# Attention powers turned by VectorE's 32x32 blocks and a scratch in device memory instead of TensorE transposes

## Chip, cores and metric

One core of a Trainium2 chip. The metric is the device time of one execution in microseconds; the time before is the median of three runs.

## The reference, cut to what matters

One decoder layer on x of 512 positions and 1024 channels, in float32. The normed input is projected at once into nine parts: queries, keys and values of 8 heads of 64 (with a gate), a pooling branch and a spatial gating branch (each with a gate). Of attention this matters:

```
logits = (q . k) * scale + bias(distance)      # own block of 256 causal, earlier block where selected
probs  = softmax(logits)                        # exp(logits - max) / sum
out    = probs . v                              # per head, 512 x 64
y      = concat(out_a * silu(g_a), pooled * silu(g_b), gated * silu(g_c)) @ w_out
```

Then the residual, a per-layer input embedding times a sigmoid gate, and a final norm.

## The kernel before, in words

Every float32 product is made of three matmuls of rounded parts ("hi" and "lo"). Weights come as chunks of 128x1024, fetched by `fetch` (L102) into three buffers `raw`; ScalarE makes the `hi` part (L128) and VectorE the `lo` part (L116), and 24 matmuls use one chunk. `ORDER` (L30) lists the projections; `through` runs them one by one and calls `tick` after each five matmuls. A tick advances every side chain by one step, and the attention loop by 1.4 steps on average (`RATE`).

Attention works on 32 tiles: 8 heads `h` times 4 blocks `i` of 128 queries, with n = 128 (i + 1) keys. In turn s of the loop in `attention` (L481), three steps long, tile s gets its scores (two matmuls into a PSUM bank, L408), the lowest logit (`lowest`, VectorE) and the powers (`powers`: exponentials on ScalarE, their sums by the same instruction). Tile s - 1 is divided by its sum (`normalise`: addition, reciprocal, multiplication on VectorE, L444 to L446). Tile s - 4 (`LAG`) is turned: i + 1 transposes of 128x128 by TensorE against `flip` (L457; `flip` also reverses the queries, which were projected in reverse order), a copy from PSUM into `ph` by ScalarE (L460), and the rest `pl` by VectorE (L116). When a head's four tiles are turned, `weigh` (L463) multiplies them with the values in eight matmuls into `ps_o`, and a copy and an addition put the head's output into `y`.

```
for j in range(n):
    nc.tensor.transpose(ps[:, j * P:(j + 1) * P], probs[h, i][:, j * P:(j + 1) * P], flip)
...
nc.scalar.activation(ph[:, :n, iq], src, AF.Copy)
```

The eight gate projections come last in the order. Their Silu, and the product of gate and branch, wait in side chains (`gate`, L613); `part` (L695) multiplies all gates but the last with two chunks of `w_out`, and only then the last one, so that the last gate has time. The order on each engine is set by the framework from the order of the code and from what it takes to be ready; engines work through their own order without skipping. All transfers but one half of the last output go through SP's queue. Tiles with the tag `t` (`temp`) share 15 buffers, the powers two buffers for each i.

Of the kernel before, what the change touches and what calls it, by code (L numbers as in the profile page):

```python
# [23 lines left out]
HD = 64  # L24
# [6 lines left out]
UNIT = 5  # L31
WARM = 14
PM = 4
LAG = 4
HELD = 5
RATE = 1.4
SS_AT = 2
# [15 lines left out]
def trunk(ctx: ExitStack, tc: tile.TileContext, t: dict, out: bass.AP):  # L53
    nc = tc.nc
    pool = lambda name, **k: ctx.enter_context(tc.tile_pool(name=name, **k))
    const = pool("const", bufs=1)
    wp = pool("wp", bufs=3)
    big = pool("big", bufs=1)
    gen = pool("gen", bufs=15)
    small = pool("small", bufs=4)  # L60
    dram = pool("dram", bufs=1, space=bass.MemoryType.DRAM)
    pm = pool("pm", bufs=PM, space=bass.MemoryType.PSUM)
    pa = pool("pa", bufs=8 - PM, space=bass.MemoryType.PSUM)
# [25 lines left out]
    def run(mms):  # L89
        for m in mms:  # L90
# [7 lines left out]
    stream = ([t["wv"][c] for c in range(4)] + [w for z, m in order for w in chunks[z](m)]  # L98
              + [t["wo"][m] for m in range(KD)] + [t["wpg"][e, c] for e in range(2) for c in range(4)])
    raws, parts, used = [], [], [0]  # L100

    def fetch(upto):  # L102
        while len(raws) < min(upto, len(stream)):
            raw = wp.tile([P, 1024], F32, tag="raw", name=f"raw_{len(raws)}")
            nc.sync.dma_start(raw, stream[len(raws)])
            raws.append(raw)

    last_parts, lows = [], []
# [48 lines left out]
        nc.sync.dma_start(xk[k], t["xT"][k])  # L157
    ident = const.tile([P, P], F32, name="ident")
    make_identity(nc, ident)
    flip = const.tile([P, P], F32, name="flip")  # L160
    nc.gpsimd.memset(flip, 0.0)
    nc.gpsimd.affine_select(flip, flip, pattern=[[1, P]], compare_op=ALU.not_equal, fill=1.0, base=-(P - 1), channel_multiplier=1)
    half = const.tile([P, 4], F32, name="half")
    nc.vector.memset(half, -0.5)
    ones = const.tile([P, 1], F32, name="ones")
# [67 lines left out]
    bias = []  # L233
# [85 lines left out]
    for g in range(4):  # L319
        r = slice((g % 2) * HD, (g % 2 + 1) * HD)  # L320
# [19 lines left out]
        nc.vector.reciprocal(icnt, icnt)  # L340


    qk, probs, sums, score, heads, yat = {}, {}, {}, {}, {}, {}

    def project(name):
        wh, wl = take()
# [52 lines left out]

    lim = 0.5 * BIG * 256.0 / math.sqrt(HD)  # L400

    def scores(h, i):
        qs, kh, kl = qk[h // 2][h % 2]
        n = P * (i + 1)
        nn = max(n, 256)
        ps = bank(pa, f"ps_s{h}{i}")
        iq = slice(i * P, (i + 1) * P)
        nc.tensor.matmul(ps[:, :nn], qs[:, iq], kh[:, :nn], start=True, stop=False)  # L408
        nc.tensor.matmul(ps[:, :nn], qs[:, iq], kl[:, :nn], start=False, stop=True)  # L409
        sc = gen.tile([P, n], F32, tag=f"p{i}", name=f"s_{h}{i}", bufs=2)  # L410
        st = small.tile([P, 8], F32, tag="st", name=f"st_{h}{i}", bufs=8)
        probs[h, i], sums[h, i] = sc, st
        score[h, i] = ps
        if i >= 2:
            gs = gen.tile([P, 256], BF16, tag="junk", name=f"gs_{h}{i}", bufs=2)
            nc.scalar.activation(gs, ps[:, :256], AF.Copy, accum_out=st[:, 2:3])
# [13 lines left out]

    def powers(h, i):
        n = P * (i + 1)
        sc, st = probs[h, i], sums[h, i]
        if i < 2:
            nc.scalar.activation(sc[:, :n], sc[:, :n], AF.Exp, bias=st[:, 0:1], scale=-1.0, accum_out=st[:, 1:2])  # L435
        else:
            nc.scalar.activation(sc[:, :256], sc[:, :256], AF.Exp, bias=st[:, 6:7], scale=-1.0, accum_out=st[:, 1:2])
            nc.scalar.activation(sc[:, 256:n], sc[:, 256:n], AF.Exp, bias=st[:, 0:1], scale=-1.0, accum_out=st[:, 7:8])  # L438

    def normalise(h, i):  # L440
        n = P * (i + 1)
        sc, st = probs[h, i], sums[h, i]
        if i >= 2:
            nc.vector.tensor_tensor(st[:, 1:2], st[:, 1:2], st[:, 7:8], op=ALU.add)  # L444
        nc.vector.reciprocal(st[:, 2:3], st[:, 1:2])
        nc.vector.tensor_scalar(sc[:, :n], sc[:, :n], st[:, 2:3], None, op0=ALU.mult)  # L446

    def turn(h, i):
        if i == 0:
            heads[h] = [big.tile([P, NT, 512], F32R, tag=n, name=f"{n}_{h}") for n in ("ph", "pl")]  # L450
            for z in heads[h]:
                nc.gpsimd.memset(f(z[:, 3, 256:384]), 0.0)  # L452
        ph, pl = heads[h]
        n = i + 1
        ps = bank(pa, f"ps_t{h}{i}")
        for j in range(n):
            nc.tensor.transpose(ps[:, j * P:(j + 1) * P], probs[h, i][:, j * P:(j + 1) * P], flip)  # L457
        src = ps[:, :n * P].rearrange("p (j q) -> p j q", q=P)
        iq = slice(i * P, (i + 1) * P)
        nc.scalar.activation(ph[:, :n, iq], src, AF.Copy)  # L460
        return low(ph[:, :n, iq], pl[:, :n, iq], src)

    def weigh(h):  # L463
        ph, pl = heads[h]
# [12 lines left out]

        nc.scalar.activation(y[r], ps[o], AF.Copy)
        return lambda: nc.vector.tensor_tensor(y[r], ps[r], y[r], op=ALU.add)

    def attention():  # L481
        tiles = [(h, i) for h in range(HEADS) for i in range(NT)]
        at = lambda d: tiles[d] if 0 <= d < len(tiles) else None
        add = None
        for s in range(len(tiles) + LAG + 2):
            while at(s) and len(qk.get(at(s)[0] // 2, [()])[0]) < 3:
                yield
            part = turn(*at(s - LAG)) if at(s - LAG) else None
            if add:
                add()  # L490
                add = None
            yield
            if at(s - LAG - 1) and (s - LAG) % NT == 0:
                add = weigh(at(s - LAG - 1)[0])
            if at(s):
                scores(*at(s))
            if at(s - 1):
                normalise(*at(s - 1))
            if part:
                part()  # L500
            if at(s):
                lowest(*at(s))
            yield
            if at(s):
                powers(*at(s))
            progress[0] = s + 1
            yield
# [100 lines left out]


    yh, yl = {}, {}  # L610
    y4, held, busy, credit = [], [], [], [0]

    def gate(c):  # L613
        ps, mms = project(f"g{c}")
# [90 lines left out]
    ps = [bank(pm, f"ps_h{m}") for m in range(2)]  # L705
# [94 lines left out]
    i = NT - 1  # L800
# [95 lines left out]
```

## Time and profile before

| what | value |
|---|---|
| median of 3 runs | 297.73 us (297.4 to 298.9) |
| profiled execution | 298.0 us |
| its span, first to last instruction | 296.0 us |
| mean granted TensorE clock | 0.995 |
| TensorE / VectorE / ScalarE / GpSimd busy | 286.5 / 204.3 / 178.0 / 34.0 us |
| moved by DMA | 33.26 MB, mean 112 GB/s |

PE is TensorE's matmuls, PEld its weight loads, DVE VectorE, ACT ScalarE, POOL GpSimd, SPq SyncE's queue of DMA issues. L457 is line 457 of the kernel. A tile's buffer numbers are left out, so `ps_t` is all of `ps_t00` to `ps_t73`. Matmuls overlap, so their durations sum to more than the time that they take.

### The profile page before, as it was taken

How to read it: one execution, taken by the hardware profiler on the slowest of the kernel's cores; microseconds unless marked ns; L12 is line 12 of the kernel's file. 1: busy time of each engine (PE TensorE's matmuls, PEld its weight loads, DVE VectorE, ACT ScalarE, POOL GpSimd, SP SyncE). 2: the span in 40 equal slices, each digit the busy share in tenths (PEclk: the TensorE clock that was granted, in tenths of full speed). 3: DMA queues.
4: the chain of work that ended last, by engine and by line, in shares of the span. 5: the costliest groups of instructions: out<-in, count | busy, mean ns of one | idle time of the engine just before them, and what ended most of it. 6: DMA issues, size and time to landing. Idle time of an engine off the chain costs nothing.

```text
span 296.0 us, 4201 instructions
## 1 busy us (share of the span) xinstructions
PE 286.5 (97%) x1436; PEld 240.1 (81%) x1436; DVE 204.3 (69%) x498; ACT 178.0 (60%) x364; POOL 34.0 (11%) x81
## 2 busy tenths in 40 slices
PE   8998999999999999999999999999999999999990
PEld 6876788788889988888888888888888888888890
DVE  2799798667987799978968858562654452355464
ACT  4895584567775756656699999651432332475221
POOL 2591132000001210000000000000000000051021
PEclk9999999999999999999999999999999999999998
DMA  6969734422222042222222222265233323400033
GB/s 177 331 235 267 290 116 144 142 71 71 74 72 73 0 144 71 74 71 73 71 71 71 74 72 71 73 207 218 83 132 95 117 71 117 132 36 3 1 141 142
DMA packets 12933, 33.26 MB, mean 112 GB/s; under 512 B 1896, under 2 KB 2664, under 8 KB 12912
## 3 DMA queue, kind: packets, MB, share of 16 engines
q1 hardware_dynamic: 12768, 32.74, 33.0%
q8 instruction: 11, 0.18, 0.3%
q10 hardware_dynamic: 144, 0.26, 0.2%
q14 instruction: 10, 0.08, 0.1%
HBM read 30.87 MB, written 2.12 MB: 111 GB/s over the span
## 4 chain that ended last, share of the span: by engine, by line
PE 69%; DVE 11%; ACT 9%; issue 4%; POOL 2%; DMA 2%; SPq 1%; POOLq 0%; DVEq 0%; ACTq 0%
PE ps_g L81 9%; PE ps_g L80 9%; PE ps_g L79 9%; PE ps_h L81 5%; PE ps_h L80 5%; PE ps_h L79 5%; ACT kh L388 2%; PE ps_t L457 2%; DMA x<-in_xT 2%; DVE lo L116 2%; ACT hi L128 1%; PE ps_o L474 1%; PE ps_o L473 1%; PE ps_s L409 1%; PE ps_u L81 1%
## 5 line engine op out<-in xcount | busy, mean ns | idle before, releaser
L128 ACT ACTIVATE hi<-raw 128x1024 fp32r<-128x1024 f32 x40 | 42.1, 1054 | 40.8 <-issue 29.8
L116 DVE TENSOR_TENSOR lo<-raw,hi 128x1024 fp32r<-128x1024 f32 x40 | 48.9, 1222 | 10.0 <-ACT hi L128 9.6
L81 PE MATMUL ps_g<-hn_hi,lo 128*128 128x512 f32 x64 | 25.6, 400 | 0.0
L80 PE MATMUL ps_g<-hn_lo,hi 128*128 128x512 f32 x64 | 25.4, 396 | 0.0
L79 PE MATMUL ps_g<-hn_hi,hi 128*128 128x512 f32 x64 | 25.3, 396 | 0.0
L79 PE MATMUL ps_g<-hi,h_hi 128*128 128x512 f32 (+1 forms) x52 | 19.9, 382 | 0.0
L701 DVE TENSOR_TENSOR h<-ps_h,h 128x512 f32<-128x512 f32 x8 | 5.5, 691 | 20.5 <-PE ps_h L81 20.5
L81 PE MATMUL ps_g<-hi,h_lo 128*128 128x512 f32 (+1 forms) x52 | 19.5, 374 | 0.0
L80 PE MATMUL ps_g<-lo,h_hi 128*128 128x512 f32 (+1 forms) x52 | 19.4, 373 | 0.0
L116 DVE TENSOR_TENSOR pl<-ps_t,ph 128x128 fp32r<-128x128 f32 (+3 forms) x32 | 15.5, 483 | 0.4
L460 ACT ACTIVATE ph<-ps_t 128x128 fp32r<-128x128 f32 (+3 forms) x32 | 13.7, 427 | 2.9 <-PE ps_t L457 2.6
L452 POOL MEMSET ph<- 128x128 f32 x8 | 1.9, 233 | 112.1 <-PE ps_o L473 73.9
L80 PEld LDWEIGHTS ps_g<-hn_lo,hi 128*128 128x128 f32 x64 | 12.0, 188 | 2.3
L457 PE MATMUL ps_t<-flip,s 128*128 128x128 f32 x80 | 13.9, 272 | 0.0
L81 PEld LDWEIGHTS ps_g<-hn_hi,lo 128*128 128x128 f32 x64 | 12.0, 188 | 2.2
L79 PEld LDWEIGHTS ps_g<-hn_hi,hi 128*128 128x128 f32 x64 | 12.1, 188 | 2.1
L80 PE MATMUL ps_v<-lo,hn_hi 128*128 128x512 f32 x32 | 12.7, 398 | 0.6 <-DVE lo L116 0.5
L438 ACT ACTIVATE s<-s,st 128x128 f32<-128x128 f32 (+1 forms) x16 | 7.2, 451 | 10.0 <-DVE st L428 9.8
L435 ACT ACTIVATE s<-s,st 128x128 f32<-128x128 f32 (+1 forms) x16 | 7.2, 453 | 9.9 <-DVE st L423 9.9
L457 PEld LDWEIGHTS ps_t<-flip,s 128*128 128x128 f32 x80 | 10.4, 140 | 3.0
L763 POOL TENSOR_SCALAR fg<-fg 128x1024 f32<-128x1024 f32 x1 | 3.8, 3810 | 77.7 <-ACT hi L128 77.7
L446 DVE TENSOR_SCALAR s<-s,st 128x128 f32<-128x128 f32 (+3 forms) x32 | 12.2, 384 | 0.7
(227 smaller groups left out, 860.6 us busy)
## 6 DMA issues: line engine op xcount, KB each, us to landing
raw<-in_wg SPq DMA_DIRECT2D x8, 512.0 KB, 3.3
raw<-in_wo SPq DMA_DIRECT2D x8, 512.0 KB, 3.3
raw<-in_wpg SPq DMA_DIRECT2D x8, 512.0 KB, 3.3
x<-in_xT SPq DMA_DIRECT2D x8, 256.0 KB, 5.3
raw<-in_wv SPq DMA_DIRECT2D x4, 512.0 KB, 5.8
bias<-tab_d SPq DMA_DIRECT2D x8, 256.0 KB, 6.1
raw<-in_wq SPq DMA_DIRECT2D x4, 512.0 KB, 6.8
raw<-in_wk SPq DMA_DIRECT2D x4, 512.0 KB, 3.3
```

Of the source, the lines that this page charges most:

```text
L79: return [lambda: nc.tensor.matmul(ps, lh, rh, start=first, stop=False), lambda: nc.tensor.matmul(ps, lh, rl, start=False, stop=False), la ...
L80: lambda: nc.tensor.matmul(ps, lh, rl, start=False, stop=False),
L81: lambda: nc.tensor.matmul(ps, ll, rh, start=False, stop=last)]
L116: return lambda: nc.vector.tensor_tensor(lo, raw, f(hi), op=ALU.subtract)
L128: nc.scalar.activation(hi, raws[j], AF.Copy)
L388: nc.scalar.activation(kh[e][r[z]], ps[r[e]], AF.Copy)
L435: nc.scalar.activation(sc[:, :n], sc[:, :n], AF.Exp, bias=st[:, 0:1], scale=-1.0, accum_out=st[:, 1:2])
L438: nc.scalar.activation(sc[:, 256:n], sc[:, 256:n], AF.Exp, bias=st[:, 0:1], scale=-1.0, accum_out=st[:, 7:8])
L446: nc.vector.tensor_scalar(sc[:, :n], sc[:, :n], st[:, 2:3], None, op0=ALU.mult)
L457: nc.tensor.transpose(ps[:, j * P:(j + 1) * P], probs[h, i][:, j * P:(j + 1) * P], flip)
L460: nc.scalar.activation(ph[:, :n, iq], src, AF.Copy)
L701: nc.vector.tensor_tensor(ht[m], ps, ht[m], op=ALU.add)
```

## The change

TensorE's transposes, `flip` and the bank `ps_t` go. A new `place` (turn s - 1) lets VectorE transpose each 32x32 block of the powers in place of the block, into a tile `turned`; four DMAs on SP's queue, one for each 32 partitions, write the blocks to their turned places in a scratch `turn_d` in device memory, in pieces of 32 floats. A new `back` (turn s - 2) reads the turned tile into the buffer of the powers. `turn` (now s - 5) then copies from there into `ph`, and the rest into `pl`; `ph` and `pl` are made once and not for each head.

The powers are not divided any more. The sums of a head (`recips`) are inverted together after its fourth tile, written to `sums_d` in device memory and read back as `shares`, one row of 512 spread over 64 partitions. `weigh` puts the queries back in order while it copies and adds (the reversed access `back`), and after the second head of a pair one multiplication of 128x512 by `shares` divides both heads' outputs. `weigh` is emitted ahead of `turn` in its loop turn. From the start to the end of attention, weights are fetched on GpSimd's queue instead of SP's.

```
-LAG = 4
+LAG = 5
...
-            nc.sync.dma_start(raw, stream[len(raws)])
+            (nc.gpsimd if busy else nc.sync).dma_start(raw, stream[len(raws)])
...
-    flip = const.tile([P, P], F32, name="flip")
...
+    sums_d = dram.tile([HEADS, S], F32, name="sums_d")
+    recips, shares = {}, {}
+    at_row = {(h, i): P * (10 * h + i * (i + 1) // 2) for h in range(HEADS) for i in range(NT)}
+    turn_d = dram.tile([P * 10 * HEADS, P], F32, name="turn_d")
...
-            nc.scalar.activation(sc[:, :n], sc[:, :n], AF.Exp, bias=st[:, 0:1], scale=-1.0, accum_out=st[:, 1:2])
+            nc.scalar.activation(sc[:, :n], sc[:, :n], AF.Exp, bias=st[:, 0:1], scale=-1.0, accum_out=rs[:, i:i + 1])
...
-    def normalise(h, i):
+    def place(h, i):
         n = P * (i + 1)
-        sc, st = probs[h, i], sums[h, i]
-        if i >= 2:
-            nc.vector.tensor_tensor(st[:, 1:2], st[:, 1:2], st[:, 7:8], op=ALU.add)
-        nc.vector.reciprocal(st[:, 2:3], st[:, 1:2])
-        nc.vector.tensor_scalar(sc[:, :n], sc[:, :n], st[:, 2:3], None, op0=ALU.mult)
+        sc = probs[h, i]
+        turned = temp(f"turned_{h}{i}")[:, :n]
+        nc.vector.transpose(turned, sc[:, :n])
+        for a in range(4):
+            nc.sync.dma_start(bass.AP(tensor=turn_d.tensor, offset=turn_d.offset + at_row[h, i] * P + 32 * a,
+                                      ap=[[P, 32], [32 * P, n // 32], [1, 32]]),
+                              turned[32 * a:32 * a + 32].rearrange("r (b c) -> r b c", c=32))
+        if i == NT - 1:
+            rs = recips[h]
+            nc.vector.tensor_tensor(rs[:, 2:4], rs[:, 2:4], rs[:, 4:6], op=ALU.add)
+            nc.vector.reciprocal(rs[:, :NT], rs[:, :NT])
+            nc.sync.dma_start(bass.AP(tensor=sums_d.tensor, offset=sums_d.offset + h * S, ap=[[1, P], [P, NT]]), rs[:, :NT])
+            if h % 2 == 0:
+                shares[h // 2] = temp(f"shares_{h // 2}")
+            nc.sync.dma_start(shares[h // 2][(h % 2) * HD:(h % 2 + 1) * HD],
+                              bass.AP(tensor=sums_d.tensor, offset=sums_d.offset + h * S, ap=[[0, HD], [1, S]]))
+
+    def back(h, i):
+        n = P * (i + 1)
+        nc.sync.dma_start(probs[h, i][:, :n].rearrange("p (j q) -> p j q", q=P),
+                          turn_d[at_row[h, i]:at_row[h, i] + n].rearrange("(j p) q -> p j q", p=P))
 
     def turn(h, i):
...
-        ps = bank(pa, f"ps_t{h}{i}")
-        for j in range(n):
-            nc.tensor.transpose(ps[:, j * P:(j + 1) * P], probs[h, i][:, j * P:(j + 1) * P], flip)
-        src = ps[:, :n * P].rearrange("p (j q) -> p j q", q=P)
+        src = probs[h, i][:, :n * P].rearrange("p (j q) -> p j q", q=P)
...
-        nc.scalar.activation(y[r], ps[o], AF.Copy)
-        return lambda: nc.vector.tensor_tensor(y[r], ps[r], y[r], op=ALU.add)
+        back = lambda ap: ap.rearrange("p (i q) -> p i q", q=P)[:, :, ::-1]
+        fore = lambda ap: ap.rearrange("p (i q) -> p i q", q=P)
+        nc.scalar.activation(fore(y[r]), back(ps[o]), AF.Copy)
+
+        def add():
+            nc.vector.tensor_tensor(fore(y[r]), back(ps[r]), fore(y[r]), op=ALU.add)
+            if e == 1:
+                nc.vector.tensor_tensor(fore(y), fore(y), back(shares[m]), op=ALU.mult)
+        return add
...
-                normalise(*at(s - 1))
+                place(*at(s - 1))
+            if at(s - 2):
+                back(*at(s - 2))
```

## Rows read from the trace of the kernel before

**Rows 1.** The page's first part: engine, busy us, share of the span, instructions

```profile
PE 286.5 (97%) x1436; PEld 240.1 (81%) x1436; DVE 204.3 (69%) x498; ACT 178.0 (60%) x364; POOL 34.0 (11%) x81
```

**Rows 2.** Windows of attention: busy us (instructions) by engine, clock, DMA share, GB/s

```profile
80.00:100.00 20.00, 20.00 (x144) 18.83 (x142) 16.41 (x55) 14.22 (x39) 2.03 (x6) 1.00 0.17 54
100.00:120.00 20.00, 19.94 (x111) 16.94 (x110) 18.29 (x59) 13.28 (x36) 1.88 (x6) 1.00 0.24 80
120.00:140.00 20.00, 20.00 (x105) 16.89 (x105) 16.86 (x54) 11.35 (x32) 0.70 (x4) 1.00 0.26 80
160.00:180.00 20.00, 20.00 (x101) 16.66 (x100) 15.17 (x48) 19.80 (x43) 0.35 (x2) 1.00 0.23 79
```

**Rows 3.** Timeline of TensorE around four transposes: start us, duration us, instruction

```profile
111.75 0.39 PE L79 MATMUL ps_k<-hn_hi,hi 128*128 128x512 f32 x1
111.98 0.60 PE L457 MATMUL ps_t<-flip,s 128*128 128x128 f32 x4
112.33 0.47 PE L408 MATMUL ps_s<-kh,qs 128*128 128x512 f32 x1
112.64 0.40 PE L409 MATMUL ps_s<-kl,qs 128*128 128x512 f32 x1
```

**Rows 4.** Instructions of tile ps_t: duration ns min/median/max, first and last start us, forms

```profile
L457 PE MATMUL ps_t<-flip,s x80: 269/272/275, 68.0 to 192.2; 128*128 128x128 f32 x80
```

**Rows 5.** Groups by line and shape, VectorE: busy us, mean ns, idle before

```profile
L116 DVE TENSOR_TENSOR pl<-ps_t,ph 128x512 fp32r<-128x512 f32 x8 | 5.5, 683 | 0.0
...
L445 DVE RECIPROCAL st<-st 128x1 f32<-128x1 f32 x32 | 5.0, 159 | 3.5 <-ACT s L435 3.1
...
L446 DVE TENSOR_SCALAR s<-s,st 128x512 f32<-128x512 f32 x8 | 3.9, 486 | 0.2
...
L116 DVE TENSOR_TENSOR pl<-ps_t,ph 128x128 fp32r<-128x128 f32 x8 | 2.3, 286 | 0.2
...
L446 DVE TENSOR_SCALAR s<-s,st 128x128 f32<-128x128 f32 x8 | 2.2, 280 | 0.1
```

**Rows 6.** The score matmuls, by their line: columns as in rows 4

```profile
L408 PE MATMUL ps_s<-kh,qs x32: 278/338/477, 55.1 to 178.5; 128*128 128x256 f32 x16, 128*128 128x384 f32 x8, 128*128 128x512 f32 x8
```

**Rows 7.** Timeline of ScalarE, a copy from PSUM and one from SBUF

```profile
105.34 0.36 ACT L460 ACTIVATE ph<-ps_t 128x256 fp32r<-128x256 f32 x1
...
108.92 0.40 ACT L535 ACTIVATE vns<-vn 128x256 fp32r<-128x256 f32 x1
```

**Rows 8.** Windows filled by pieces of 1 KB, 512 B and 256 B

```profile
2.00:3.00 1.00, 1.00 (x6) 0.69 (x5) 0.00 (x0) 0.07 (x1) 0.28 (x1) 1.00 0.75 233
35.50:36.00 0.50, 0.50 (x4) 0.40 (x3) 0.50 (x2) 0.22 (x1) 0.00 (x0) 1.00 0.13 33
...
41.50:42.00 0.50, 0.50 (x4) 0.42 (x3) 0.50 (x2) 0.50 (x2) 0.26 (x1) 1.00 0.15 31
```

**Rows 9.** Issues on SP's queue, pw_raw and bias: columns of rows 4

```profile
L321 SPq DMA_DIRECT2D pw_raw<-in_pw x4: 472/594/595, 38.4 to 40.2; - x4
...
L236 SPq DMA_DIRECT2D bias<-tab_d x8: 337/430/820, 21.6 to 25.5; - x8
```

**Rows 10.** DMA issues: count, KB each, median us from issue to landing

```profile
raw<-in_wg SPq DMA_DIRECT2D x8, 512.0 KB, 3.3
...
pw_raw<-in_pw SPq DMA_DIRECT2D x4, 16.0 KB, 2.6
```

**Rows 11.** Timelines of TensorE and VectorE at the end of attention

```profile
195.83 0.29 PE L474 MATMUL ps_o<-pl,v 128*128 128x256 f32 x1
...
201.97 0.69 DVE L116 TENSOR_TENSOR y4pl<-sg,y4ph 128x512 fp32r<-128x512 f32 x1 [0.70 <-ACT y4ph L641]
...
207.53 0.39 PE L79 MATMUL ps_h<-y4ph,hi 128*128 128x512 f32 x1
```

**Rows 12.** Timeline of ScalarE: a gate's first Silu, the last copy of powers

```profile
151.02 0.63 ACT L626 ACTIVATE sg<-sg 128x512 f32<-128x512 f32 x1
...
192.55 0.60 ACT L460 ACTIVATE ph<-ps_t 128x512 fp32r<-128x512 f32 x1 [0.26 <-PE ps_t L457]
```

More of the change, by code (lines that the diff above doesn't have):

```diff
@@ L100, in trunk @@
     raws, parts, used = [], [], [0]
+    busy = []
     def fetch(upto):
@@ L159, in trunk @@
     make_identity(nc, ident)
-    flip = const.tile([P, P], F32, name="flip")
-    nc.gpsimd.memset(flip, 0.0)
-    nc.gpsimd.affine_select(flip, flip, pattern=[[1, P]], compare_op=ALU.not_equal, fill=1.0, base=-(P - 1), channel_multiplier=1)
     half = const.tile([P, 4], F32, name="half")
@@ L340, in prepare @@
         nc.vector.reciprocal(icnt, icnt)
-    qk, probs, sums, score, heads, yat = {}, {}, {}, {}, {}, {}
+    qk, probs, sums, score, heads, yat = {}, {}, {}, {}, [], {}
     def project(name):
@@ L413, in scores @@
         score[h, i] = ps
+        if i == 0:
+            recips[h] = small.tile([P, 6], F32, tag="rs", name=f"rs_{h}", bufs=3)
         if i >= 2:
@@ L432, in powers @@
         n = P * (i + 1)
-        sc, st = probs[h, i], sums[h, i]
+        sc, st, rs = probs[h, i], sums[h, i], recips[h]
         if i < 2:
-            nc.scalar.activation(sc[:, :n], sc[:, :n], AF.Exp, bias=st[:, 0:1], scale=-1.0, accum_out=st[:, 1:2])
+            nc.scalar.activation(sc[:, :n], sc[:, :n], AF.Exp, bias=st[:, 0:1], scale=-1.0, accum_out=rs[:, i:i + 1])
         else:
-            nc.scalar.activation(sc[:, :256], sc[:, :256], AF.Exp, bias=st[:, 6:7], scale=-1.0, accum_out=st[:, 1:2])
-            nc.scalar.activation(sc[:, 256:n], sc[:, 256:n], AF.Exp, bias=st[:, 0:1], scale=-1.0, accum_out=st[:, 7:8])
@@ L440, in normalise @@
-    def normalise(h, i):
+            nc.scalar.activation(sc[:, :256], sc[:, :256], AF.Exp, bias=st[:, 6:7], scale=-1.0, accum_out=rs[:, i:i + 1])
+            nc.scalar.activation(sc[:, 256:n], sc[:, 256:n], AF.Exp, bias=st[:, 0:1], scale=-1.0, accum_out=rs[:, i + 2:i + 3])
+    def place(h, i):
         n = P * (i + 1)
-        sc, st = probs[h, i], sums[h, i]
-        if i >= 2:
-            nc.vector.tensor_tensor(st[:, 1:2], st[:, 1:2], st[:, 7:8], op=ALU.add)
-        nc.vector.reciprocal(st[:, 2:3], st[:, 1:2])
-        nc.vector.tensor_scalar(sc[:, :n], sc[:, :n], st[:, 2:3], None, op0=ALU.mult)
+        sc = probs[h, i]
[14 more added lines that the diff above has]
+                              bass.AP(tensor=sums_d.tensor, offset=sums_d.offset + h * S, ap=[[0, HD], [1, S]]))
@@ L448, in turn @@
+    def back(h, i):
+        n = P * (i + 1)
+        nc.sync.dma_start(probs[h, i][:, :n].rearrange("p (j q) -> p j q", q=P),
+                          turn_d[at_row[h, i]:at_row[h, i] + n].rearrange("(j p) q -> p j q", p=P))
     def turn(h, i):
-        if i == 0:
-            heads[h] = [big.tile([P, NT, 512], F32R, tag=n, name=f"{n}_{h}") for n in ("ph", "pl")]
-            for z in heads[h]:
+        if not heads:
+            heads.extend(big.tile([P, NT, 512], F32R, tag=n, name=f"{n}_heads") for n in ("ph", "pl"))
+            for z in heads:
@@ L452, in turn @@
                 nc.gpsimd.memset(f(z[:, 3, 256:384]), 0.0)
-        ph, pl = heads[h]
+        ph, pl = heads
         n = i + 1
-        ps = bank(pa, f"ps_t{h}{i}")
-        for j in range(n):
-            nc.tensor.transpose(ps[:, j * P:(j + 1) * P], probs[h, i][:, j * P:(j + 1) * P], flip)
-        src = ps[:, :n * P].rearrange("p (j q) -> p j q", q=P)
+        src = probs[h, i][:, :n * P].rearrange("p (j q) -> p j q", q=P)
         iq = slice(i * P, (i + 1) * P)
@@ L463, in weigh @@
     def weigh(h):
-        ph, pl = heads[h]
+        ph, pl = heads
         m, e = h // 2, h % 2
@@ L487, in attention @@
                 yield
-            part = turn(*at(s - LAG)) if at(s - LAG) else None
             if add:
@@ L491, in attention @@
                 add = None
-            yield
             if at(s - LAG - 1) and (s - LAG) % NT == 0:
                 add = weigh(at(s - LAG - 1)[0])
+            part = turn(*at(s - LAG)) if at(s - LAG) else None
+            yield
             if at(s):
@@ L610, in trunk @@
     yh, yl = {}, {}
-    y4, held, busy, credit = [], [], [], [0]
+    y4, held, credit = [], [], [0]
     def gate(c):
```

## The prediction

> **What bounds the kernel now.** I read the page first, for each engine's share of the span: TensorE is at 97%, VectorE at 69%, ScalarE at 60%, GpSimd at 11% [rows 1]. A share is an average, so next came the windows of the stretch in which attention is interleaved with the projections. There TensorE is busy 19.94 to 20.00 of every 20 us at a granted clock of 1.00, VectorE 15.2 to 18.3, ScalarE 11.4 to 19.8, and the DMA engines are busy 0.17 to 0.26 of the time [rows 2]. The reader should see that TensorE has no gap there, and that VectorE between 100 and 120 us is the next one up. A busy TensorE can still hide waits, so third I took the timeline of single matmuls around one group of transposes: neighbours start 0.23 us apart and nothing waits [rows 3]. So in this stretch time goes with TensorE's work, and each instruction taken from it is worth its cadence, as long as nothing else becomes later than it.
>
> **The 80 transposes go.** Their mean busy time of 272 ns [rows 4] overlaps with neighbours and is not what they cost. In [rows 3] the 512-column matmul before the group starts at 111.75, the four transposes at 111.98, the first score matmul at 112.33 and the second at 112.64. From the group's start to that second start are 0.66 us; without the group it would be the 0.23 us of one 512-column matmul. Four transposes cost 0.43 us, one 0.1075 us, and 80 cost 8.6 us. All lie between 68 and 192 us, where TensorE is the bound, so the whole 8.6 us counts.
>
> **VectorE.** Per head the edit removes four normalising multiplications (0.28 us at 128 columns to 0.49 at 512, evenly stepped: 4 x 0.385 = 1.54 us), four reciprocals of 0.16 us and two additions of one column taken alike, together 2.5 us [rows 5]. It adds four block transposes, one addition, one reciprocal and half of a 128x512 multiplication. No row shows a VectorE transpose. Below, it can't be expected under the multiplication of the same shape, 1.54 us for the four; above, I take the two-input subtraction of the same four shapes, 0.29 to 0.68 us, 4 x 0.485 = 1.94 us [rows 5]. The rest is 0.16 + 0.16 + 0.69/2, or 0.67 us, where 0.69 us stands for a two-input operation of 512 columns. So VectorE changes by -0.3 to +0.1 us a head; I take 0. It matters in one place. The score matmuls of 32 tiles start between 55.1 and 178.5 us [rows 6], 3.98 us a tile; 100 to 120 us holds five tiles, and TensorE loses 5 x 2.5 x 0.1075 = 1.3 us there. That leaves 18.7 us for 18.3 us of VectorE work with waits in order. I count those 1.3 us as given back.
>
> **ScalarE.** Its 32 copies of the powers read SBUF instead of PSUM: 0.40 instead of 0.36 us for 256 columns [rows 7], 1.3 us in all, hidden in its idle 30%. Only 160 to 180 us has no such cover (19.80 of 20 busy [rows 2]); eight copies there would be late by 0.3 us, and TensorE, at 20.00 busy, already runs past that crowding. I take 0.
>
> **The way through device memory.** A tile of n columns leaves as four DMAs of n pieces of 128 B each and returns as n pieces of 512 B. A head has n = 128 + 256 + 384 + 512 = 1280, so 5120 pieces out and 1280 back, or 320 and 80 on each of 16 engines. A head takes 4 x (3.98 - 0.27) = 14.8 us once the transposes are gone. No row has a 128 B write to device memory. The nearest are short windows in which one sort of transfer runs [rows 8], busy share x 16 x length over bytes moved: 256 B pieces 1.2 us over 61, or 20 ns; 512 B 1.04 us over 32, or 32 ns; 1 KB 12 us over 228, or 53 ns. From below I take 10 ns, half of the 256 B row; from above the 1 KB row's 53 ns; my value is 20 ns, the nearest row in size. Weights take 0.225 of the time (mean of [rows 2]), 3.3 us a head. The engines' work per head is then 320 x 0.020 + 80 x 0.032 + 3.3 = 12.3 of 14.8 us: it fits, at 83%. The break-even is (14.8 - 5.9)/320 = 28 ns a piece. By the Trainium skill (DMA: Bandwidth & Descriptors, Specifications) a transfer needs 512 B or more for full rate, and below that the engine reads, modifies and writes. No run here shows that for a write; read as a doubled piece it is the first rival.
>
> **SP's queue.** A head costs it 16 + 4 issues, one for the sums and one for the shares. Issues of transfers that cover only some partitions last 0.59 us, the bias loads 0.43 us [rows 9]; 22 of them are 9.5 to 13.0 us of 14.8. A tile's return waits for its writes, with the next tile's four issues (2.4 us) in between, while small transfers land 2.6 us after issue [rows 10]; the wait is nearly covered. The weights' issues leave this queue, which is why it can hold that. On GpSimd's queue they meet an engine busy 34 us in all [rows 1]; behind a fetch that waits for its buffer stand only the tiny variance steps. Weights land in 3.3 us [rows 10] and one chunk feeds 24 matmuls of 0.23 us, 5.5 us; with three buffers a landing 2 us later stays hidden. If that cover were gone, the 18 chunks behind the first four names of the order would cost 36 us at 2 us each.
>
> **Latency and the longer lag.** From the exponential to the copy: transpose 0.7, four issues 2.4, landing 2.6, issue 0.6, landing 3.3, together 9.6 us. In the code the copy comes five tiles later, 18.5 us. The lag of 5 instead of 4 moves the last head behind the last gate. Before, its matmuls end at 196.0, the last gate's low part at 202.7, and the matmuls that read it start at 207.5 [rows 11]: 5 us of cover, of which this takes some 3 us with the added multiplication. I take 0.
>
> **Sum.** The profiled execution took 298.0 us, 296.0 of it span, 0.27 above the median of 297.73. 298.0 - 8.6 + 1.3 = 290.7, so on the median's level 290.4 us. With VectorE at its best and nothing given back it would be 287.
>
> **Rivals.**
> (a) Pieces too dear: the DMA engines become the bound, and copies on ScalarE wait for the return. At twice 20 ns a head needs 18.7 us, 3.9 more than it has, 31 us over eight heads: 322 us (a piece that costs a reading and a writing would do this). It decides from 28 ns on; at the top of the bound it would be far worse (22.9 us a head, 355 us). For it: 83% is already little room, with writes arriving in bursts. Against it: the rows fall steadily with size, from 53 to 32 to 20 ns. This ends on the other side. Chance 0.20.
> (b) SP's queue as the bound: 13.0 us of issues plus one uncovered landing a head (the shares' read waits for the sums' write, 2.6 us) is 15.6 us, 0.8 too much, 6 us in all: 297 us, no change. Against it: other issues can stand between. Chance 0.13.
> (c) Order on ScalarE: the code's order isn't the engine's. The first gate's Silu, which the code emits after the whole of attention, runs at 151.0, and the last copy of the powers at 192.6 [rows 12]. A copy can thus be placed as early as two tiles after its exponential; then the round trip of 9.6 us has 7.4 us, and each pair of tiles loses 2.2 us, 35 us in 16 pairs: 325 us. Three tiles (11.1 us) would cover it, so it decides between two and three. Chance 0.17.
>
> **How the numbers follow.** My forecast, TensorE stays the bound, has 0.50 with its own range of 287 to 294. Within 0.5% of the median (296.2 to 299.2, about what a measurement of this kernel can tell from no change) lies (b), 0.13. Slower are (a) and (c), 0.37. The range that leaves out about 2 in 10, half of (a) and (c) with a little below, is 287 to 320.
>
> **What would show it.** Right: no transposes, TensorE busy some 278 us without gaps between 60 and 190, score starts 3.7 us apart, DMA busy share near 0.8 there, and no wait of the copy on a DMA among the longest. Wrong by (a): DMA share at 1 and landings that grow from head to head. By (b): SP issuing without pause and the return's issue late while the engines are idle. By (c): ScalarE idle in front of its copies with DMA share well under 1. A VectorE transpose far above 0.68 us at 512 columns would make VectorE the bound between 80 and 140 us.

## The result, and the profile after

The changed kernel takes 352.97 us (median of 4 runs, 349.45 to 355.84) against 297.56 for the kernel before on the same chip: 1.1815 times as long (95% interval 1.1716 to 1.1913). The forecast was 290.4 in a range of 287 to 320. Medians here and below are of all executions, while ratios leave out those disturbed by the chip's slower state, as the profiled one of 355.84 us is, so differences of medians and of ratios part by up to 2 us.

The page's first part, its lines of TensorE's clock and of the bytes moved in 40 slices, the chain, and the two groups that belong together:

```profile
PE 296.1 (84%) x1356; PEld 245.6 (69%) x1356; DVE 207.0 (58%) x470; ACT 177.9 (50%) x362; POOL 38.1 (11%) x89
...
PEclk9999999999599985669996699996989999999998
...
GB/s 199 367 207 312 97 121 122 123 129 26 153 139 17 260 77 94 9 69 186 135 56 128 120 126 151 52 183 99 170 214 77 185 64 117 98 140 2 1 85 152
...
PE 38%; DMA 16%; DVE 5%; ACT 4%; issue 4%; SPq 2%; POOL 0%; POOLq 0%; DVEq 0%; ACTq 0%
...
L493 PE MATMUL ps_o<-ph_heads,v 128*128 128x256 f32 (+2 forms) x32 | 14.4, 454 | 35.2 <-ACT ph_heads L480 35.2
L480 ACT ACTIVATE ph_heads<-s 128x128 fp32r<-128x128 f32 (+3 forms) x32 | 14.7, 464 | 48.0 <-DMA s<-turn_d 47.3
```

TensorE is at 84% instead of 97% [rows 1]. ScalarE's copies of the powers waited 47.3 us for returns (`s<-turn_d`), and the head products behind them kept TensorE idle for 35.2 us. The bytes moved have holes: 26, 17 and 9 GB/s where the neighbours have 69 to 260. So the DMA engines were not swamped by bytes; either something stopped them, or nothing was issued.

Windows of attention, columns as in [rows 2]:

```profile
80.00:100.00 20.00, 10.62 (x46) 8.96 (x45) 11.52 (x30) 9.10 (x20) 1.05 (x2) 0.74 0.63 102
100.00:120.00 20.00, 20.00 (x135) 18.42 (x133) 13.91 (x44) 10.46 (x27) 4.77 (x11) 1.00 0.52 108
120.00:140.00 20.00, 9.85 (x39) 8.06 (x38) 12.20 (x37) 11.00 (x29) 0.79 (x2) 0.75 0.75 108
140.00:160.00 20.00, 13.95 (x52) 11.55 (x51) 6.92 (x17) 1.59 (x4) 0.00 (x0) 0.66 0.51 58
...
180.00:200.00 20.00, 8.50 (x34) 6.93 (x33) 10.41 (x30) 7.10 (x18) 1.05 (x2) 0.70 0.82 113
```

No compute engine is near its limit in the bad windows (of 20 us, lines 1, 3, 4 and 5), and the DMA engines are busy 0.51 to 0.82 of the time; VectorE and ScalarE have less to do than before. The granted clock, 1.00 throughout before, is 0.66 to 0.75 in the windows where TensorE stood still. The waits are thus paid for again in part, by matmuls at the lower level (1.2 instead of 2.4 GHz) after them: the same 1356 matmuls keep TensorE busy for 296.1 us here and for 277.1 in a kernel without such waits (below).

What stopped it is seen in SP's own timeline (start, duration of the issue, line):

```profile
74.99 1.93 SPq L453 DMA_DIRECT2D turn_d<-turned  x4
77.03 0.45 SPq L460 DMA_DIRECT2D sums_d<-rs  x1
89.05 0.38 SPq L468 DMA_DIRECT2D s<-turn_d  x1
89.47 0.51 SPq L463 DMA_DIRECT2D shares<-sums_d  x1
```

and, three heads later, in the chain of waits, with two matmuls soon after it that are alike but for the clock:

```profile
133.63 0.25 SPq L460
...
134.06 16.12 DMA s<-turn_d
...
150.20 0.64 ACT ph_heads L480
...
150.88 0.80 PE ps_o L493
...
155.18 0.43 PE ps_u L80
...
158.46 0.23 PE ps_u L80
```

L460 is the write of a head's inverted sums: 2 KB, but as 512 pieces of 4 B, one for each partition and block. After it, 11.6 us pass until the next return is issued; at 134.06 a return issued right behind it takes 16.12 us to land. The transposes of VectorE are not to blame: 296, 431, 570 and 702 ns by width on average, 2.00 us for the four, a little above the upper bound of 1.94.

### The profile page after: what moved, and what is told of

It is laid out like the page before. It is cut to its first block, busy times and chain, and to the rows that moved or that the text cites. A ratio compares the mean times of both kernels' runs of the same rounds, so it can differ in the third digit from the quotient of the medians.

```text
span 354.1 us, 4338 instructions
## 1 busy us (share of the span) xinstructions
PE 296.1 (84%) x1356; PEld 245.6 (69%) x1356; DVE 207.0 (58%) x470; ACT 177.9 (50%) x362; POOL 38.1 (11%) x89
## 4 chain that ended last, share of the span: by engine, by line
PE 38%; DMA 16%; DVE 5%; ACT 4%; issue 4%; SPq 2%; POOL 0%; POOLq 0%; DVEq 0%; ACTq 0%
DMA s<-turn_d 12%; PE ps_g L79 6%; PE ps_g L80 6%; PE ps_g L81 6%; PE ps_h L80 4%; DMA turn_d<-turned 3%; PE ps_h L81 3%; PE ps_h L79 3%; PE ps_o L493 2%; SPq L453 2%; PE ps_o L494 2%; DMA sums_d<-rs 1%; ACT ph_heads L480 1%; PE ps_u L80 1%; PE ps_u L81 1%
## 5 line engine op out<-in xcount | busy, mean ns | idle before, releaser
L493 PE MATMUL ps_o<-ph_heads,v 128*128 128x256 f32 (+2 forms) x32 | 14.4, 454 | 35.2 <-ACT ph_heads L480 35.2
L480 ACT ACTIVATE ph_heads<-s 128x128 fp32r<-128x128 f32 (+3 forms) x32 | 14.7, 464 | 48.0 <-DMA s<-turn_d 47.3
L117 DVE TENSOR_TENSOR pl_heads<-s,ph_heads 128x128 fp32r<-128x128 f32 (+3 forms) x32 | 15.4, 484 | 38.2 <-ACT ph_heads L480 38.0
L493 PEld LDWEIGHTS ps_o<-ph_heads,v 128*128 128x128 f32 x32 | 8.5, 267 | 38.6 <-ACT ph_heads L480 38.1
L451 DVE STREAM_TRANSPOSE turned<-s 128x128 f32<-128x128 f32 (+3 forms) x32 | 15.6, 500 | 7.1 <-ACT s L443 3.4
L79 PE MATMUL ps_h<-y4ph,hi 128*128 128x512 f32 x32 | 12.7, 408 | 2.4 <-ACT y4ph L670 2.4
L494 PE MATMUL ps_o<-pl_heads,v 128*128 128x256 f32 (+2 forms) x32 | 14.0, 445 | 0.2 <-DVE pl_heads L117 0.2
L80 PE MATMUL ps_h<-y4pl,hi 128*128 128x512 f32 x32 | 13.2, 413 | 0.6 <-DVE y4pl L117 0.6
L81 PE MATMUL ps_h<-y4ph,lo 128*128 128x512 f32 x32 | 12.9, 404 | 0.0
```

Source lines behind the costliest of these rows:

```text
L79: return [lambda: nc.tensor.matmul(ps, lh, rh, start=first, stop=False), lambda: nc.tensor.matmul(ps, lh, rl, start=False, stop=False), la ...
L80: lambda: nc.tensor.matmul(ps, lh, rl, start=False, stop=False),
L81: lambda: nc.tensor.matmul(ps, ll, rh, start=False, stop=last)]
L117: return lambda: nc.vector.tensor_tensor(lo, raw, f(hi), op=ALU.subtract)
L451: nc.vector.transpose(turned, sc[:, :n])
```

## Experiments

All kernels were timed against the kernel before on the same chip (297.7 to 297.9).

**The sums' write.** Theory S says that it is the cause; rivals are the weights on GpSimd's queue (Q) and the pieces of 128 B. First without the write:

```
-            nc.sync.dma_start(bass.AP(tensor=sums_d.tensor, ..., ap=[[1, P], [P, NT]]), rs[:, :NT])
...
-                              bass.AP(tensor=sums_d.tensor, offset=sums_d.offset + h * S, ap=[[0, HD], [1, S]]))
+                              bass.AP(tensor=t["fg"].tensor, offset=t["fg"].offset, ap=[[0, HD], [1, S]]))
```

> The changed kernel without the write of the inverted sums (512 pieces of 4 B per head); the shares are read from the final gain instead, so the division is by other numbers. Theory S (the write of the sums holds up the transfers behind it, some 12 us a head in the trace of the changed kernel): the waits of the copies on the return fall from 47 us to a few and the time is 290 to 302 us. Rival P (the 128 B pieces of the powers are too dear): at most a few us better, 343 to 352. Rival Q (weights on GpSimd's queue): the same, 343 to 352.

Measured 314.42 us, 1.0587 (1.0548 to 1.0626), above the 290 to 302 of S. 38.6 of the 62.6 us between forecast and result are this one write (36.5 by the ratios; the interval of the changed kernel's ratio alone is 3 us to either side); some 24 stay. Returns of 256 KB now land in 3.0 us (5.5 in the changed kernel), those of 192 KB in 3.6 (13.1).

Next the write as four rows of 512 B, the sums turned by TensorE first:

```
+            pr = bank(pa, f"ps_r{h}")
+            nc.tensor.transpose(pr[:NT, :P], rs[:, :NT], ident)
+            rt = temp(f"rt_{h}")[:NT, :P]
+            nc.vector.tensor_copy(rt, pr[:NT, :P])
+            nc.sync.dma_start(sums_d[h:h + 1].rearrange("o (i q) -> (o i) q", q=P), rt)
```

> The changed kernel with the inverted sums of a head turned by one small TensorE transpose and written as four rows of 512 B, so 4 pieces instead of 512; 8 transposes, 8 small copies more. Theory S: 290 to 303 us, within 3 us of the kernel without the write. Rivals P and Q: 343 to 355.

321.34 us, 1.0795 (1.0740 to 1.0850): the same 2 KB in 4 pieces instead of 512 save 31.6 us. That is 6.9 us more than without any write, where S allowed 3; so most of the 38.6 us goes with the count of pieces, not all. The changed kernel with its weights on SP:

```
-            (nc.gpsimd if busy else nc.sync).dma_start(raw, stream[len(raws)])
+            nc.sync.dma_start(raw, stream[len(raws)])
```

> The changed kernel with all weights fetched on SP's queue again. Rival Q: clearly better, 300 to 325 us. Theory S and rival P: not better, 350 to 375, since the weights now stand behind the same held-up transfers and behind SP's waits.

346.38 us, 1.165 (1.1617 to 1.1684): 6.6 us better (4.9 by the ratios) and outside both forecasts, so Q is no more than a small part. And the write, with the read of the shares that nothing uses, added to the kernel before:

```
+        if i == NT - 1:
+            nc.sync.dma_start(bass.AP(tensor=sums_d.tensor, ..., ap=[[1, P], [P, NT]]), st[:, 3:7])
...
```

> The kernel before with one thing added: after a head's fourth tile four columns are written to device memory as 512 pieces of 4 B and read back over 64 partitions, into a tile that nothing uses. Theory S: each write takes about 10 us to land, the weights behind it on SP's queue are late, and the time rises by 10 to 60 us. Rival P (such a write costs like any small transfer, some 3 us): landing under 4 us and no change, 296 to 300 us.

297.07 us, 0.9987 (0.9964 to 1.0010): no change, so S was right on the landing and wrong on the time. But here the write is seen by itself, in the lines of DMA by slice and of DMA issues (KB each, median us to landing):

```profile
DMA  6969634322040316040421324076233213300033
GB/s 189 334 248 280 253 118 143 142 71 71 3 161 2 99 26 200 1 160 3 160 71 16 76 80 152 2 270 245 89 126 108 105 71 129 128 30 2 2 140 142
...
shares<-sums_d SPq DMA_DIRECT2D x8, 128.0 KB, 3.1
...
sums_d<-st SPq DMA_DIRECT2D x8, 2.0 KB, 10.0
```

2 KB land in 10.0 us. Meanwhile slices fall to 1 to 3 GB/s, where weights before ran at a steady 71 to 75, with DMA busy shares of 0. These slices alone do not show that the write holds other transfers: here everything goes through SP's queue, and SP stands still at the read of the shares until the write has landed (77.1 us in eight waits), so next to nothing else is issued. But one fetch, of `in_wu`, was issued between a write (at 100.51) and its read (at 111.89), at 101.65 us. Its landing here, and that of the same weights in the kernel before:

```profile
raw<-in_wu SPq DMA_DIRECT2D x2, 512.0 KB, 11.6
```

```profile
raw<-in_wu SPq DMA_DIRECT2D x2, 512.0 KB, 3.3
```

The trace has the landing of this one of the two alone: 11.6 us. The DMA engines are busy for 0.16 of the time from 100.4 to 112 us. What is caught behind the write waits, and the time does not show as busy time. It costs nothing here, since the weights have three buffers of cover. In the changed kernel the powers' own way goes through the same engines.

**Which part of the write holds the others?** It could be the read that waits for it in a queue (SQ), or the pieces on the DMA engines (SE). Write and read of the shares on ScalarE's queue:

```
-            nc.sync.dma_start(bass.AP(tensor=sums_d.tensor, ...), rs[:, :NT])
+            nc.scalar.dma_start(bass.AP(tensor=sums_d.tensor, ...), rs[:, :NT])
...
-            nc.sync.dma_start(shares[h // 2][(h % 2) * HD:(h % 2 + 1) * HD],
+            nc.scalar.dma_start(shares[h // 2][(h % 2) * HD:(h % 2 + 1) * HD],
```

> The changed kernel (353.0 us) with the whole computation; only the write of the inverted sums in pieces of 4 B and the read of the shares are issued by ScalarE instead of SP. If the sums' write costs by standing ahead of the returns in one queue (theory SQ): the returns no longer wait, 300 to 322 us, and the write itself still takes some 10 us to land. If it holds the DMA engines themselves (rival SE), the returns come as late as before: 340 to 355 us.

367.75 us, 1.2349, worse than either theory had it: the engine that issues the read stands still until the write has landed. Waits of ScalarE in that kernel (us in total, times, longest):

```profile
ACT ph_heads L480 <- DMA sums_d<-rs: 29.8, 4, 8.4
...
ACT pool_x L606 <- DMA sums_d<-rs: 10.4, 1, 10.4
ACT vns L564 <- DMA sums_d<-rs: 8.8, 1, 8.8
...
ACT y L500 <- DMA sums_d<-rs: 8.0, 1, 8.0
```

So read and write were taken apart: the read (now in a function `share`) three turns later, the write on GpSimd's queue, and, in a second kernel, left on SP's.

```
+            if at(s - 4) and at(s - 4)[1] == NT - 1:
+                share(at(s - 4)[0])
...
-            nc.sync.dma_start(bass.AP(tensor=sums_d.tensor, ...), rs[:, :NT])
+            nc.gpsimd.dma_start(bass.AP(tensor=sums_d.tensor, ...), rs[:, :NT])
```

> The changed kernel (353.0 us), whole computation; the sums' write in 4 B pieces is issued by GpSimd, and the shares are read (by SP) three turns after it instead of at once, so that no queue waits for the write's landing. VectorE's order is early there. Theory SQ (the queue and the read that waits in it are the cost): 298 to 318 us, SP's waits for `sums_d` gone. Rival SE (512 pieces hold the DMA engines themselves): 330 us or more, returns still 10 us and more in landing.

> As the run before, but the write stays on SP's queue; only the read of the shares is moved three turns later. If it was the read's wait on SP that held the queue: 300 to 320 us, equal to the run with the write on GpSimd within 5 us. If transfers behind the write in its queue also stand, 325 to 350, and returns issued behind a write of the sums land some 10 us later than the others.

339.24 us (1.1386) and 331.58 us (1.1121). The late read gains 21.4 us. Most of that was the queue standing still, but not shown to be all: the late read also changes VectorE's order, and further below it gains 3.0 us without the write and 8.5 with the write as four rows. The other queue gains nothing; it is 7.7 us slower, and why is not shown. The chain of the first of them, with the write issued by GpSimd at 74.17:

```profile
74.03 0.50 SPq L453
...
74.57 11.74 DMA turn_d<-turned
...
86.39 7.64 DMA s<-turn_d
...
94.12 0.64 ACT ph_heads L482
```

and two windows of it, before and in the write (columns as above):

```profile
60.00:74.00 14.00, 14.00 (x65) 11.70 (x64) 10.28 (x32) 10.12 (x26) 1.05 (x2) 1.00 0.53 131
75.00:86.00 11.00, 10.70 (x55) 8.93 (x53) 10.26 (x34) 7.77 (x21) 1.83 (x3) 1.00 0.98 65
```

A write of turned blocks on SP's queue, issued about when GpSimd's write starts, lands 11.74 us later (1.8 us for the two issued just before), though the sums' write is not in SP's queue at all. The transfers caught show as busy, 0.98 of the time at half the bytes. Both parts are real: SE first, SQ on top. The Trainium skill says so much (DMA: Bandwidth & Descriptors, Issuing engines are not separate DMA queues): transfers of all issuing engines run on the same 16 DMA engines. The trace agrees, with these 11.74 us.

**The other 24 us: too few buffers?** Theory T: `turned` and `shares` use up the 15 buffers `t`. Block transposes in place instead of into `turned`, the 13-buffer kernel before, and two buffers of its own for `turned`:

```
-        turned = temp(f"turned_{h}{i}")[:, :n]
-        nc.vector.transpose(turned, sc[:, :n])
+        nc.vector.transpose(sc[:, :n], sc[:, :n])
+        turned = sc[:, :n]
```

> The run without the sums' write (314.4 us), and VectorE turns the blocks in place: no tile `turned`, the four DMAs read the powers' own buffer. Left out as there: the sums' write. Theory T (the rest of that run's loss comes from the 15 buffers `t`, which `turned` and `shares` now share with the side chains, so that allocations wait and engines that work in order stand still): PE's gaps at 114 to 120, 157 to 164 us go, the queue's waits for `turned` fall from 48 us to under 15, and the time falls to 293 to 302 us. Rival L (the way through device memory itself is what comes late: landings and waits between writes and returns): 310 to 318 us, PE's gaps stay. Rival V (an in-place transpose costs VectorE more or orders it worse): above 318.

> The run with the sums turned by TensorE and written as four rows of 512 B (321.3 us), and VectorE turns the blocks in place; the whole computation is done. Theory T: 297 to 306 us (the run in place without the sums' write, and the sums' small way added, some 4 us at most). Rival L: 316 to 323.

```
-    gen = pool("gen", bufs=15)
+    gen = pool("gen", bufs=13)
```

> The kernel before with 13 buffers `t` instead of 15, nothing else. Theory T, two buffers are about what `turned` and `shares` take at a time: slower, by 5 us or more (303 us and up). Rival L: the 15 are not used to the last one, 297 to 299 us. A result between says that the buffers carry a part.

The same line, and in `place`:

```
-        turned = temp(f"turned_{h}{i}")[:, :n]
+        turned = gen.tile([P, 512], F32, tag="turned", name=f"turned_{h}{i}", bufs=2)[:, :n]
```

> The run without the sums' write, with `turned` in two buffers of its own and 13 instead of 15 for `t`: the same memory, divided. Theory T in its first form (too few buffers in all): 310 us or more, as before. Theory T in its second form (a ring of 15 is passed round in order, and 32 short-lived tiles more turn it to a long-lived one sooner): falls to 293 to 305. Rival L: 310 to 318 as well, so this run tells only the two forms of T apart, and the run in place tells T from L.

In this order 311.91 us (1.048), 319.28 (1.0712), 297.97 (1.0006) and 315.94 (1.0592). Two buffers less change nothing, and transposing in place saves 2.1 to 2.5 us, at the edge of the noise. T falls.

**VectorE's order?** In the run in place TensorE's longest waits are for `vns` (5.36 us) and `pooled_h` (6.18), not for the copies. In VectorE's program these steps stand late: the second pooling step 37 instructions behind the first, 5 before the change. Theory O takes this for the loss. Four kernels on the base in place without the sums' write: writes issued by ScalarE; `RATE` 1.2 instead of 1.4; no way through device memory at all; the writes without the returns.

```
-            nc.sync.dma_start(bass.AP(tensor=turn_d.tensor, ...
+            nc.scalar.dma_start(bass.AP(tensor=turn_d.tensor, ...
```

> The run in place without the sums' write (311.9 us; left out as there: the sums' write), and the four writes of a tile are issued by ScalarE instead of SP; no work is taken away. Theory O: with four writes a tile on SP's queue the framework places VectorE's `vn` steps of blocks 2 and 3 and the second pooling step late in VectorE's order (37 instructions after the first pooling step, 5 before the change), and TensorE, whose order does not know it, waits 5.5 and 6.3 us for them and then runs at half clock. In this kernel the second step stands 2 instructions behind the first: the two gaps go, 292 to 300 us. Rival W (the round trip through memory itself comes late, whoever issues it): 308 to 318 us. If ScalarE, which issues 128 transfers, becomes late, its copies show it and the time stays above 305 with other gaps.

```
-RATE = 1.4
+RATE = 1.2
```

> The same base (311.9 us, the sums' write left out), and attention advances 1.2 instead of 1.4 steps a tick; every transfer stays on its queue. VectorE's order has the `vn` and pooling steps early again here too. Theory O: the gaps at `vns` and `pooled_h` go, 293 to 303 us; the later end of attention may give some of it back in the tail. Rival W: 306 to 316, the gaps only move.

```
-        for a in range(4):
-            nc.sync.dma_start(bass.AP(tensor=turn_d.tensor, ...
...
-        nc.sync.dma_start(probs[h, i][:, :n].rearrange("p (j q) -> p j q", q=P), ...
+        pass
```

> The same base, and neither the writes of the turned blocks nor the returns: left out is the way through device memory (and the sums' write), the block transposes and everything else stay. Both O and W: 288 to 294 us, near the predicted 290.4 (the sum without any cost of the way). If it stays above 300, the cost lies in VectorE's transposes, the longer lag or the multiplication by the shares, and both theories fall.

Of these two removals the second alone:

> The run in place without the sums' write (311.9 us), and without the returns: left out are the returns (the copies read the block-transposed powers directly) and the sums' write; the four writes a tile stay, and nothing waits for their data. VectorE's order is as late there as in that run: the second pooling step 42 instructions behind the first. Theory O (the order, and not the way): 300 to 312 us, with TensorE's waits for `vns` and `pooled_h` as long as there. Rival W (the returns come late): 288 to 294, as without the whole way (290.0).

328.73 us (1.1049), 307.67 (1.0289), 290.00 (0.9756, 0.9719 to 0.9793) and 294.51 (0.9895). The first says little: ScalarE waited some 24 us for its own writes. In the second the two gaps are gone, but not the loss: counted by matmuls, it starts its 840th 0.6 us later than the writes alone and its 960th 13.7 later, so the loss moved to the tail. The last two settle the places. With the writes alone VectorE's order is as late and the cost is 4.5 us; the returns add 17.4.

The kernel without the way, its page's first part and TensorE's one wait in attention (us in total, times, longest):

```profile
PE 277.1 (96%) x1356; PEld 232.2 (81%) x1356; DVE 203.9 (71%) x470; ACT 178.1 (62%) x364; POOL 39.2 (14%) x89
...
PE ps_sg L79 <- DVE y L576: 2.1, 1, 2.1
```

TensorE's waits for the two late steps with the writes alone, and with the returns as well:

```profile
PE ps_pool L79 <- ACT pooled_h L623: 3.3, 1, 3.3
PE ps_sg L79 <- DVE qs L369: 1.5, 1, 1.5
```

```profile
PE ps_pool L79 <- ACT pooled_h L624: 6.2, 1, 6.2
PE ps_sg L79 <- ACT vns L563: 5.4, 1, 5.4
```

What the writes cost is thus one wait behind the late order: counted by matmuls, they lose 3.6 us against the kernel without the way, all around the wait of 3.3 us. Lines of the DMA queues (packets, MB, share of 16 engines) of the kernels without the way, with the writes, and with both, in this order:

```profile
q1 hardware_dynamic: 9952, 21.20, 21.8%
```

```profile
q1 hardware_dynamic: 52960, 26.45, 33.8%
```

```profile
q1 hardware_dynamic: 63712, 31.70, 38.2%
```

With spans of 288.4, 292.1 and 309.3 us that is 62.9, 98.7 and 118.2 us of 16 engines. The 40,960 pieces of 128 B cost 35.8 x 16 / 40,960 = 14 ns each, the 10,240 of 512 B 19.5 x 16 / 10,240 = 30 ns.

Last, all writes and returns with an early order: the read of the shares three turns later, on the same base, and once with the whole computation (sums as four rows).

> The run in place without the sums' write (311.9 us; left out as there: the sums' write), and the shares are read three turns later. All writes and returns stay; the second pooling step stands 4 instructions behind the first in VectorE's order (37 there), the last two `vn` steps 6 apart instead of 1. If the late order together with the returns makes the loss (theory O'): 292 to 299 us, no waits of TensorE for `vns` or `pooled_h` above 2 us. If the returns cost by themselves (W): 305 to 315, TensorE waits for copies of the powers or for what stands behind them.

> The same with the whole computation: the sums turned by TensorE, written as four rows of 512 B, the shares read three turns later, transposes in place (319.3 us with the early read). Theory O': 296 to 303 us. W: 312 to 322.

308.87 us (1.036, 1.0318 to 1.0401) and 310.83 (1.0377, 1.0274 to 1.0481), the latter between both ranges. TensorE's waits for `vns` and `pooled_h` are gone and the time is only 3.0 us less. O falls as the cause of the bulk: the loss moved to other places. TensorE's waits over 0.9 us after 100 us in the first of them (the two timelines' rows that have a wait):

```profile
157.82 0.50 PE L494 MATMUL ps_o<-ph_heads,v 128*128 128x512 f32 x1 [1.85 <-ACT ph_heads L481]
...
165.15 0.79 PE L79 MATMUL ps_g<-hn_hi,hi 128*128 128x512 f32 x1 [2.37 <-ACT sg L653]
...
204.35 0.50 PE L79 MATMUL ps_h<-yh,hi 128*128 128x512 f32 x1 [2.59 <-ACT sg L662]
...
215.38 1.65 PE L79 MATMUL ps_h<-y4ph,hi 128*128 128x512 f32 x3 [2.39 <-ACT y4ph L673]
```

```profile
160.00:180.00 20.00, 17.63 (x67) 14.34 (x66) 12.00 (x37) 14.94 (x35) 0.53 (x1) 0.74 0.64 152
...
200.00:220.00 20.00, 15.02 (x55) 11.48 (x54) 8.76 (x15) 7.99 (x14) 0.53 (x1) 0.83 0.40 131
```

Counting matmuls in the two traces shows where the 14.4 us between this run and the writes alone arise. It lies 0.6 us behind them at the 760th matmul, 7.3 at the 800th, 7.0 at the 880th and 15.0 from the 960th to the end: 6.6 us go at 157 to 166 us, 8.0 at the tail. (It is 2.4 us behind already after the first loads, before any return, and the writes alone lose that again at their own waits.) It is not the landing of the returns: neither in this trace nor in that of the run in place does the profile end a compute engine's wait with a return, where ScalarE in the changed kernel waited 47.3 us for them. What differs is the order. In TensorE's program of the kernels with returns the last head's products stand behind 36 matmuls of `part`, directly ahead of the first one that reads `y4ph` (but for the kernel with its weights on SP, 26 ahead and 9 between, and the one with the writes on ScalarE, none and 30). Without the returns none of those 36 stands ahead of them and 12 others lie between; before, 21. ScalarE's rows at the two waits of the tail:

```profile
202.41 1.28 ACT L662 ACT_TABLE_LOAD   x1
203.70 0.60 ACT L662 ACTIVATE sg<-ps_g 128x512 f32<-128x512 f32 x1
...
212.91 0.63 ACT L673 ACTIVATE y4ph<-sg 128x512 fp32r<-128x512 f32 x1 [6.41 <-PE ps_o L494]
```

At the first, TensorE waits 2.59 us for a gate's Silu behind a table load of 1.28 us. At the second, ScalarE's copies into `y4ph` wait 6.41 us for the last head's products, and TensorE then 2.39 us for the copies: the cover that the tail had is gone from the program itself. That the order makes the whole of the loss is argued and not shown; no run holds it fixed. No whole version beats the kernel before; the best is the 310.83 us.

> The run with the sums' write on GpSimd and the late read, and the block transposes in place; whole computation. Both SQ and O: the best whole version so far, 294 to 305 us; below 297.6 it would beat the kernel before. If SE holds, above 325.

This run, the one with the write on GpSimd's queue and the late read with transposes in place, took 1.1055 of the kernel before (1.0998 to 1.1112), or 329 us, and not 294 to 305. Without the write the same program has 308.87, so the 512 pieces cost 20 us even where their queue holds no return.

## Why the prediction was wrong

In steps from the result to the forecast, each the difference of two runs (in this order; in another they could come out otherwise): the sums' write 353.0 to 314.4 = 38.6 us; `turned` out of place 2.5; the returns 311.9 to 294.5 = 17.4; the writes of the blocks 294.5 to 290.0 = 4.5. Together 63.0, and what is left is 290.0 where the forecast says 290.4.

- **Transposes, VectorE, ScalarE, weights' queue: right.** The sum of these terms is the kernel without the way, 290.0 us. TensorE is busy for 277.1 us there (some 278 forecast), and this is not luck: its one wait in attention, 2.1 us at 116 us for VectorE (`y`), stands where the prediction gave back 1.3 us. VectorE's transposes came out above their upper bound (2.00 us a head instead of 1.94). The weights on GpSimd's queue are no free edit in the changed kernel (6.6 us), but a small one.
- **The way through device memory: prices right, even below.** 14 ns for a piece of 128 B (20 taken), 30 ns for one of 512 B (32 taken). Rival (a) did not happen. Of the rule of the Trainium skill weighed there (DMA: Bandwidth & Descriptors, Specifications), a read and a write for a transfer under 512 B does not show in the price of the 128 B pieces; that they stay below the full rate agrees, with 9 bytes a ns and engine against 17 for 512 B.
- **SP's queue: the step that failed.** It counts "one for the sums" and has "small transfers land 2.6 us after issue [rows 10]". The write was priced by its 2 KB and not by its 512 pieces: it lands in 10.0 us, four times as late, and delays transfers of the other queues meanwhile (11.74 us for one of 1.8). Rival (b) names the wait, "the shares' read waits for the sums' write", and prices it at the same 2.6 us; with 10 us and the other transfers held it is 38.6 us in all and the kernel is far slower, not even. The piece count was worked out for the turned blocks with care and not for the smallest transfer.
- **Latency and the longer lag: the cover held, and the returns were still not free.** The round trip was compared with five tiles of code (18.5 us), and the lag with 5 us of cover at the tail: "I take 0". Without the sums' write and in place no compute engine waits for a return, and with the lag of 5 but without the way TensorE has no wait at the tail. What the step left out is that the returns come with another order on the engines; they cost 17.4 us. In the last run without the sums' write (308.87 us, 14.4 above the writes alone) 8.0 us are lost at the tail and 6.6 at 157 to 166 us. Rival (c) had the right thought, that the code's order isn't the engine's, but put it at ScalarE's copies waiting for the return and at every pair of tiles.
- **What would show it** was of use: DMA share well under 1 and idle in front of ScalarE's copies read like (c); only SP's timeline told the sums' write apart.

Open: which places in the order cost the 6.6 us at 157 to 166 us. TensorE waits there for a copy of the powers (1.85 us), for its low part and for a gate's copy (`sg`, 2.37). The chain of waits through this stretch holds no return, but a write of the blocks that lands 5.36 us after 158.47, so late writes are not ruled out there. Early or late places of VectorE's steps only moved such waits (311.9, 308.9, 307.7 us).

## What to carry to other kernels

Price each transfer by its count of pieces, the tiny ones first: look whether the last dimension is contiguous on both sides, and if it isn't, turn the data on an engine before it leaves. Then ask what lies on the same DMA engines while it lands: the same write cost nothing where only weights with cover went by, and 38.6 us where the path itself did. A return through memory can also move where the framework puts the work around it, so compare the order of the program, at the tail above all, and not only the latency with the lag.

## What the runs showed of the hardware

- A write of 512 pieces of 4 B to device memory lands in 10.0 us, and transfers issued behind it wait: 11.6 us for a fetch in the same queue (3.3 before), 11.74 for a write in another (1.8 just before). The DMA engines are busy 0.16 of the time in the one case and 0.98 in the other, at half the bytes. The Trainium skill (DMA: Bandwidth & Descriptors, Rules for kernel authors) says that a last dimension that isn't contiguous becomes one descriptor for each element; the page of the kernel before with the write added agrees, with 6248 packets under 512 B instead of 1896, 544 for each write and its read. Why the transfers behind it wait is not shown.
- A piece of 128 B written costs 14 ns of one DMA engine, one of 512 B read back 30 ns: less for each piece, more for each byte.
- A transpose of 32x32 blocks on VectorE, float32 on 128 partitions, takes 0.30 us at 128 columns and 0.70 at 512, in place 0.31 and 0.71.
- In the 20 us windows of the changed kernel in which TensorE stood still for 6 to 11.5 us its clock was granted at 0.66 to 0.75. Matmuls behind such a wait took 0.43 us at the lower level instead of 0.23, and the same 1356 matmuls 296.1 us of busy time instead of 277.1.
